# The hand-over from an RWKV scan to the FFN behind it: last output products from SBUF in eight PSUM banks, early tiles for the next stage, and a token norm in a written order

## The chip, the cores and the metric

The kernel runs on one core of a Trainium2 chip. Its time is the device time of one execution in microseconds (us), taken as the median of several runs. One further execution was taken with the hardware profiler; the traces below are of that one.

Engines: PE is TensorE (matrix products; PEld its weight loads), DVE is VectorE, ACT is ScalarE, POOL is GpSimd, SP is the engine whose queue issues all DMAs of this kernel. PSUM has eight banks of 128 x 512 float32.

## The reference

A trunk of two layers on 512 tokens of 1024 channels. Each layer is FFN, mixer, FFN, with a layer norm behind each of the three. The mixer of layer 0 is neighbourhood attention, that of layer 1 a bidirectional RWKV-7 scan. The change lies between the mixer of layer 1 and the last FFN:

```python
def layer_norm(x, g, b):
    mu = mean(x, -1); var = mean(square(x - mu), -1)
    return (x - mu) * rsqrt(var + 1e-5) * g + b

def swiglu(x, w_in, w_out):
    gate, up = split(x @ w_in, 2)          # F = 2816
    return (silu(gate) * up) @ w_out

# end of rwkv7_bidir: y is the scan's output, 16 heads of 64 channels
y = groupnorm(y) * lnx_g + lnx_b           # over the 64 channels of each head
m = ((y + bonus) * g) @ w_out              # (512 x 1024) @ (1024 x 1024)

x = layer_norm(ALPHA * x + m, ln_g[1], ln_b[1])
x = layer_norm(ALPHA * x + 0.5 * swiglu(x, w_in, w_out), ln_g[2], ln_b[2])
```

All data are float32. Most large products are made of three float32r products (`mm3`: high x high, high x low, low x high) on operands that `split` has cut in two: an ACT copy makes the high part and a subtraction on DVE or POOL the low part.

## The kernel before

**The scan.** Class `Scan` goes through the eight head pairs in slots numbered -2 to 7. In slot n pair n runs its chain of eight steps over the time chunks, while pairs n+1 to n+3 are prepared. Each part of the work is a generator with a letter: `c` is the chain (four yields a step), `d` the outputs of a step, `x` (`finish`, pair n-1) the group norm of a finished pair, `e` (`gate`, pair n-1) its gating, `o` (`outs`) the early output products, `v` the value projection, `i`, `k`, `j` the inversion of the chunk matrices, whose long part is a series of small POOL operations. The strings in `SEQ` say in which order the generators advance in a slot. Under `manual_schedule(engines=MANUAL_SCAN)` PE, ACT and DVE execute exactly in that order; POOL and the DMA queue of SP are ordered by the scheduler, and each executes in its order.

A chain step is: PE `c` (L1204), ACT `wr` (L1205), PE `c` (L1216), ACT `vt` (L1217, L1218), PE `m` (L1222), DVE `vt` (L1224).

**The output product.** `gate` writes each pair's gated output to the DRAM tensor `d_o`. In slots 6 and 7 `outs` takes the pairs 0 to 4 (`EARLY = 5`): it loads them into `xv` (the former value input), loads the matching rows of w_out into tiles that the scan no longer needs (`ar`, `ar`, `bk`, `bk`, `wv`, in that order), multiplies (`wide`, L849: one product in two halves of 64 columns), adds ALPHA * x and stores the sums to `d_x`.

**The hand-over.** After slot 7 come `finish(7)` and `gate(7)`. Then the pools of the scan are closed and `rwkv_out` runs, ordered by the scheduler: it reloads the last three pairs from `d_o`, loads and splits the last three row blocks of w_out, reloads x from `d_x`, makes the remaining products with `mm3` (72 products, L239), and normalises the four token tiles (`residual_norm`). `to_channels` transposes each normed tile (L277) and splits it into `xT` (the "put"). In between `lead` loads and splits four units of the FFN's first weights and multiplies them with the first half of the tokens; `follow` does the second half at the head of `ffn`. The unit loads of the FFN go through two `raw` buffers, the splits' low parts are on POOL (L197), and `Winograd.sums` (L639 to L642) prepares its second weights on POOL.

Lines of the norm: L295 adds the products to x and sums the rows, L299 and L300 are the variance and its root on ACT, L303 and L306 apply mean, gain, scale and bias on DVE.

## Time and profile before

| | before |
|---|---|
| runs | 2314.69, 2315.7, 2319.5 us |
| median | 2315.7 us |
| profiled execution | 2311.64 us |
| its span, first to last instruction | 2309.9 us |
| PE busy in the span | 2169.5 us (94%) |
| POOL busy in the span | 1442.0 us (62%) |
| DVE, ACT busy | 1107.9 us (48%), 983.0 us (43%) |
| mean granted clock of TensorE | 0.973 |

How to read the rows. In the windows view each row is a stretch in us from the span's start, its length, the busy time of each engine with the number of its instructions, the granted clock of TensorE (1.00 is full speed), the share of time that the DMA engines were busy, and GB/s. In the timeline a row is start, duration, engine, line, operation, what it writes and reads, and in brackets how long the engine was idle before and what ended that. In the chain of waits a row is start, duration, and what the end of the program was waiting for just then. A group row gives minimum, median and maximum in ns. Matrix products are pipelined: the duration of one is longer than the distance between two.

### The profile page before, as it was taken

Reading aid. Unit: us, or ns where it says so; the run is one execution under the profiler, and the core shown is the slowest. Engines: PE = TensorE matmul, PEld = TensorE weight load, DVE = VectorE, ACT = ScalarE, POOL = GpSimd, SP = SyncE. Lnnn points to the kernel's source line nnn. Section 1 sums busy time; section 2 is a strip of 40 time slices with the busy share of each in tenths; the row PEclk is TensorE's granted clock in tenths of the full one; section 3 lists DMA queues with packets and bytes.
Section 4 is the critical chain, followed back from the end, with each engine's and each line's share of the span. In section 5 each row is a group of like instructions: output and inputs, shape, how many; then the busy total and the mean of one; then the engine's idle time right before and its main releaser. Section 6 shows DMA issues by size and latency. Waiting matters only on the chain. (4 is left out here: it accounts for less than half of the span.)

```text
span 2309.9 us, 35198 instructions
## 1 busy us (share of the span) xinstructions
PE 2169.5 (94%) x13808; PEld 1716.6 (74%) x13808; DVE 1107.9 (48%) x1552; ACT 983.0 (43%) x1712; POOL 1442.0 (62%) x1231
## 2 busy tenths in 40 slices
PE   8999999999999999999999878799999876999998
PEld 7888878887888887888888655445666545888886
DVE  2333357375523335723333695435887446233336
ACT  3333335376333333533333434336777423333334
POOL 6778745465568775777886532145877506578863
PEclk9999999999999999999999979799999987999999
DMA  6444453432434446344445416744545426244453
GB/s 202 138 150 146 140 197 124 126 92 79 140 114 137 141 138 226 113 134 146 143 140 191 127 56 204 255 142 121 146 126 145 132 94 211 82 147 142 141 173 119
DMA packets 351362, 330.40 MB, mean 143 GB/s; under 512 B 48554, under 2 KB 277546, under 8 KB 351196
## 3 DMA queue, kind: packets, MB, share of 16 engines
q1 hardware_dynamic: 351196, 328.15, 45.3%
q8 instruction: 108, 1.77, 0.3%
q14 instruction: 58, 0.48, 0.1%
HBM read 263.05 MB, written 48.53 MB: 135 GB/s over the span
## 5 line engine op out<-in xcount | busy, mean ns | idle before, releaser
L197 POOL TENSOR_TENSOR w<-raw,w 128x1024 fp32r<-128x1024 f32 (+2 forms) x203 | 503.7, 2482 | 311.7 <-ACT w L196 306.3
L201 PE MATMUL bank<-xT,w 128*128 128x512 f32 x1416 | 552.4, 390 | 0.0
L202 PE MATMUL bank<-xT,w 128*128 128x512 f32 x1416 | 551.6, 390 | 0.0
L203 PE MATMUL bank<-xT,w 128*128 128x512 f32 x1416 | 551.5, 389 | 0.0
L196 ACT ACTIVATE w<-raw 128x1024 fp32r<-128x1024 f32 (+1 forms) x207 | 218.7, 1057 | 337.5 <-POOL ts L639 142.2
L347 DVE SCALAR_TENSOR_TENSOR ar<-bank,tmp 128x512 f32<-128x512 f32 x88 | 60.9, 692 | 588.8 <-PE bank L203 579.4
L203 PEld LDWEIGHTS bank<-xT,w 128*128 128x128 f32 x1416 | 266.1, 188 | 55.6
L202 PEld LDWEIGHTS bank<-xT,w 128*128 128x128 f32 x1416 | 266.2, 188 | 54.0
L201 PEld LDWEIGHTS bank<-xT,w 128*128 128x128 f32 x1416 | 266.1, 188 | 54.2
L668 PE MATMUL bank<-w,ring 128*128 128x512 f32 x864 | 200.8, 390 | 9.1 <-DVE w L197 8.0
L668 PEld LDWEIGHTS bank<-w,ring 128*128 128x128 f32 x864 | 161.6, 188 | 45.8 <-DVE w L197 10.6
L668 PE MATMUL bank<-wx,an 128*128 128x512 f32 x792 | 187.3, 389 | 0.0
L1143 POOL TENSOR_TENSOR tm<-qs,zs 128x126 f32<-128x126 f32 (+22 forms) x248 | 106.9, 431 | 106.4 <-DVE qs L1136 61.3
L668 PEld LDWEIGHTS bank<-wx,an 128*128 128x128 f32 x792 | 148.7, 188 | 30.8
L197 POOL TENSOR_TENSOR wx<-ra,wx 128x512 fp32r<-128x512 f32 x132 | 168.5, 1307 | 0.0
L197 DVE TENSOR_TENSOR ring<-ar,ring 128x1024 fp32r<-128x1024 f32 x44 | 130.8, 2972 | 72.7 <-ACT ring L196 72.5
L345 ACT ACTIVATE tmp<-bank 128x512 f32<-128x512 f32 x88 | 52.6, 598 | 240.6 <-PE bank L203 240.6
L1145 POOL TENSOR_TENSOR zs<-zs,tm 128x126 f32<-128x126 f32 (+22 forms) x248 | 113.5, 458 | 19.4
L196 ACT ACTIVATE wx<-ra 128x512 fp32r<-128x512 f32 x132 | 83.1, 633 | 86.0 <-PE bank L668 68.0
L197 POOL TENSOR_TENSOR w<-late,w 128x1024 fp32r<-128x1024 f32 x28 | 70.6, 2520 | 76.2 <-ACT w L196 69.2
L201 PE MATMUL bank<-xT,ring 128*128 128x256 f32 (+1 forms) x352 | 103.3, 308 | 10.6 <-ACT xT L196 8.7
L639 POOL TENSOR_TENSOR ts<-ra 128x512 f32<-128x512 f32 x44 | 57.6, 1309 | 86.2 <-DMA ra<-in_ffn_w_out_dram 86.1
(277 smaller groups left out, 3797.1 us busy)
## 6 DMA issues: line engine op xcount, KB each, us to landing
raw<-in_ffn_w_in_dram SPq DMA_DIRECT2D x176, 512.0 KB, 3.7
ra<-in_ffn_w_out_dram SPq DMA_DIRECT2D x44, 1024.0 KB, 4.9
late<-d_late SPq DMA_DIRECT2D x30, 512.0 KB, 5.3
late<-in_ffn_w_out_dram SPq DMA_DIRECT2D x28, 512.0 KB, 4.5
raw<-in_w_qkv_dram SPq DMA_DIRECT2D x24, 512.0 KB, 3.7
d_late<-ts SPq DMA_DIRECT2D x44, 256.0 KB, 3.2
d_late<-ra SPq DMA_DIRECT2D x44, 256.0 KB, 2.0
xs<-ar SPq DMA_DIRECT2D x64, 128.0 KB, 2.3
```

The costliest lines, as they stand in the source:

```text
L196: self.nc.scalar.activation(h, raw, AF.Copy)
L197: (eng or self.nc.vector).tensor_tensor(l, raw, h.bitcast(F32), ALU.subtract)
L201: nc.tensor.matmul(out, wh, xh, start=start, stop=False)
L202: nc.tensor.matmul(out, wh, xl, start=False, stop=False)
L203: nc.tensor.matmul(out, wl, xh, start=False, stop=stop)
L345: nc.scalar.activation(s, pg, AF.Silu)
L347: nc.vector.scalar_tensor_tensor(raw[:, 3:7:3] if j else raw[:, 0:8:7], halves_of(pu), 0.5, halves_of(s), ALU.mult, ALU.mult)
L639: nc.gpsimd.tensor_tensor(t3, r[:, 1, 1], r[:, 0, 1], ALU.subtract)
L668: self.nc.tensor.matmul(acc, lhs, u[:, i], start=bool(first) and m == 0, stop=last and m == 2, skip_group_check=more)
L1143: nc.gpsimd.tensor_tensor(tv, qs[:, s, 0:s].rearrange("p (a o) -> p a o", o=1).broadcast_to([P, s, n]), zs[:, s : s + 1, c0:].broadcast_to ...
L1145: nc.gpsimd.tensor_tensor(zs[:, 0:s, c0:], zs[:, 0:s, c0:], tv, ALU.add)
```

## The change

- `outs` starts with the tile `wv`, then the two `ar` and two `bk`, and also loads the row blocks 5, 6 and 7 of w_out into three unit tiles of the scan. In `SEQ[6]` the first `o` stands behind one whole chain step and the start of the next.
- From pair 5 on `gate` leaves its result in `xv` in SBUF instead of `d_o`.
- `last` replaces the products of `rwkv_out`: the pairs 5, 6 and 7 are multiplied in plain float32 (24 products), each half of a token tile in a PSUM bank of its own, eight in all. The products of pairs 5 and 6 for the first two tiles stand ahead of the gating of pair 7.
- The tiles that the scan does not need in its last slot lie in a pool of their own (`rwe`, tags `EARLY_TAGS`) on the other side of SBUF. It is closed ahead of slot 7, and a pool `ex` is opened in its place, for x, the norm parameters, the two `raw` buffers and four weight units of the next stage. A generator `leads` (letter `w` in `SEQ[7]`) loads and splits the four leading FFN units there in slot 7; x is reloaded as soon as both halves of a tile are stored (`reload`).
- `rwkv_out` keeps only the norm, cut into four steps for each tile, in a written order for PE, ACT and DVE.
- A POOL copy that reads the last scaled tile is the `mark`: all POOL work of the FFN is ordered behind it (`issue_after`).

```diff
-    6: "c x n o o c c o o x c o c c x c d n c o c c d c x o c o c x c c x d o c o c c c d o c n o o o o o c c d k c "
+    6: "c x n c c x c c o c x c o d n o o o c o c c d c x o c o c x c c x d o c o c c c d o c n o o o o o c c d k c "
        "o o o o o c o c k c d c j c d o c c j c o o d e o",
-    7: "x c c c o x c o c c d c o c o c c c x d o c o c c d c o c o c c d c x o c o c c d x c o c o c c d x c o c e "
-       "d c c c o d",
+    7: "w x c c c o x c o c c d c o c o c c c x d o c o c w c d c o c o c c d c x w o c o c c d x c o c w o c c d x c o c e "
+       "w d c c c o d",
...
+EARLY_TAGS = ("k", "iv", "r", "lw", "kz", "a2r", "a2u", "v", "vr", "qc", "qd", "zs", "qs", "tm")
...
     def raw(self):
-        return self.sb_w.tile([P, 1024], F32, name="raw", tag="raw", bufs=self.nraw)
+        return self.home(self.sb_w).tile([P, 1024], F32, name="raw", tag="raw", bufs=self.nraw)
...
-    def rwkv_out(self, x, o, w_out, ln, lead):
-        oT = self.new_xT()
-        units = []
-        for c in range(EARLY, ND):
-            raw = self.tmp()
-            self.nc.sync.dma_start(raw, o[:, c, :])
-            self.split(*oT.get(c), halves_of(raw))
-            units.append(self.load_unit(w_out[c * P : (c + 1) * P, :], None, True, self.nc.vector))
-        self.load_x(x)
-        params = self.ln_params(ln)
...
+    def rwkv_out(self, acc, params, lead):
+        self.spare.append(self.ring())
         nxt = self.new_xT()
...
+        banks = [(self.bank(), self.bank()) for _ in range(NT)]
+        def norm(t):
+            y, yn = self.x[t], [self.tmp() for _ in range(2)]
+            s0, s1, mu, va, rs, self.mark = self.small("st", 6)
+            for h, sm in zip(range(2), (s0, s1)):                       # sum step
+                stt(y[:, hs[h]], y[:, hs[h]], 1.0, acc[t][h], ALU.mult, ALU.add, accum_out=sm)
+            nc.vector.tensor_scalar(mu, s0, s1, -1.0 / D, ALU.add, ALU.mult)
+            nc.scalar.activation(self.junk.bitcast(BF16), y, AF.Square, bias=mu, accum_out=va)
+            nc.scalar.activation(rs, va, AF.Sqrt, scale=1.0 / D, bias=self.eps)
+            yield
+            for h in range(2):                                          # mean step
+                stt(yn[h], y[:, hs[h]], mu, gbc[:, hs[h]], ALU.add, ALU.mult)
+            yield
+            nc.vector.reciprocal(rs, rs)                                # scale step
+            for h in range(2):
+                stt(y[:, hs[h]], yn[h], rs, bbc[:, hs[h]], ALU.mult, ALU.add)
+            yield
+            self.to_channels(t, y, nxt, banks[t])                       # transposes and put
+            yield
...
+        with self.tc.manual_schedule(engines=MANUAL_SCAN):
+            order(0, 0, 1, 0, 1, 0, 1)
+            order(2, 1, 2)
+            parts = self.lead(lead, nxt)
+            next(parts)
+            order(2, 3, 3, 2, 3)
+            self.mark = nc.gpsimd.tensor_copy(self.mark, self.x[3][:, 0:1])
+            next(parts)
+            order(3)
         return nxt
...
+                if n == HEADS // 2 - 1:
+                    self.early.tile([P, 56], F32, name="pad")
+                    self.opened.close()
+                    late.enter_context(self.k.early())
+                    self.lw = self.leads(lead, ln)
                 self.slot(n)
-            list(self.finish(HEADS // 2 - 1))
-            list(self.gate(HEADS // 2 - 1))
+            self.ending = self.finish(HEADS // 2 - 1)
+            next(self.ending)
+    def leads(self, lead, ln):
+        k, nc = self.k, self.nc
+        nc.sync.dma_start(self.w[ND - 1], self.w_out[(ND - 1) * P :, :])
+        k.x = [k.ex.tile([P, D], F32, name=f"x{t}", tag="x", bufs=NT) for t in range(NT)]
+        self.params = k.ln_params(ln)
...
+        load(0)
+        load(1)
+        self.reload()
+        yield
+        for i in range(LEAD):
+            u = k.ring().rearrange("p (i f) -> p i f", i=2)
+            k.split(u[:, 0, :], u[:, 1, :], raws[i], nc.gpsimd)
...
+            if i + 2 < LEAD:
+                load(i + 2)
+            yield
+    def reload(self):
+        while self.k.ex and self.stored >= 2:
+            t = NT - len(self.left)
+            self.nc.sync.dma_start(self.k.x[t], self.left.pop(0))
+            self.stored -= 2
+    def last(self):
...
+        def add(t, h, cs):
+            if cs[0] == EARLY:
+                acc[t, h] = self.k.bank()
+            for c in cs:
+                nc.tensor.matmul(acc[t, h], self.xv[:, c, t * P : (t + 1) * P], self.w[c][:, h * 512 : (h + 1) * 512],
+                                 start=c == EARLY, stop=c == hp)
+        with self.k.tc.manual_schedule(engines=MANUAL_SCAN):
+            list(self.ending)
+            for t, h in ((0, 0), (0, 1), (1, 0), (1, 1)):
+                add(t, h, (EARLY, EARLY + 1))
+            list(self.gate(hp, "bank"))
+            add(2, 0, (EARLY, EARLY + 1))
+            for t, h in ((0, 0), (0, 1), (1, 0), (1, 1), (2, 0)):
+                add(t, h, (hp,))
+            for t, h in ((2, 1), (3, 0), (3, 1)):
+                add(t, h, (EARLY, EARLY + 1, hp))
...
-        w = [self.tile(n, [P, NC, 2, CH], 2).rearrange("p a b c -> p (a b c)") for n in ("ar", "ar", "bk", "bk")]
-        w += [self.tile("wv", [P, ND, P]).rearrange("p a b -> p (a b)"),
-              self.units[self.taken[5, 1][0]][0].rearrange("p a b c d -> p (a b c d)")]
+        w = [self.tile("wv", [P, ND, P]).rearrange("p a b -> p (a b)")]
+        w += [self.tile(n, [P, NC, 2, CH], 2).rearrange("p a b c -> p (a b c)") for n in ("ar", "ar", "bk", "bk")]
+        w += [self.units[i][0].rearrange("p a b c d -> p (a b c d)") for i in (2, 4, 3)]
...
-        nc.vector.scalar_tensor_tensor(bon, bon, k.col(C_XB, hp), g, ALU.add, ALU.mult)
-        nc.sync.dma_start(self.dram["o"][:, hp, :], bon)
+        early = hp < EARLY
+        nc.vector.scalar_tensor_tensor(bon if early else self.xv[:, hp, :], bon, k.col(C_XB, hp), g, ALU.add, ALU.mult)
+        if early:
+            nc.sync.dma_start(self.dram["o"][:, hp, :], bon)
...
+            with tc.issue_after(k.mark.ins):
+                k.ffn(xT, ffn_w_in[1, 1], ffn_w_out[1, 1], 5, lambda: None)
```

More of the change, by code (lines that the diff above doesn't have):

```diff
@@ L100, in __init__ @@
         self.nc = tc.nc
+        self.ex, self.spare = None, []
         nc = self.nc
@@ L216, in lead @@
     def lead(self, cols, xT):
-        us = [self.load_cols(w, c0, True) for w, c0 in cols]
+        us = [u if isinstance(u, bass.AP) else self.load_cols(*u, True) for u in cols]
         self.led = us, [self.bank() for _ in us], xT
@@ L595, in rwkv_project, with order @@
                 store(dram["g"][:, c, :], pp)
[L597 to L620 removed]
+    def rwkv_out(self, acc, params, lead):
+        self.spare.append(self.ring())
+        nxt = self.new_xT()
+        nc = self.nc
+        gbc, bbc = params
+        hs = [slice(h * 512, (h + 1) * 512) for h in range(2)]
+        stt = nc.vector.scalar_tensor_tensor
+        banks = [(self.bank(), self.bank()) for _ in range(NT)]
[17 more added lines that the diff above has]
+            yield
+        def order(*ts):
+            for t in ts:
+                next(ns[t])
+        self.junk = self.tmp()
+        ns = [norm(t) for t in range(NT)]
+        with self.tc.manual_schedule(engines=MANUAL_SCAN):
[7 more added lines that the diff above has]
+            order(3)
@@ L925, in take, with run @@
         return self.units[i]
-    def run(self):
+    def run(self, late, lead, ln):
         with self.k.tc.manual_schedule(engines=MANUAL_SCAN):
@@ L1264, in outs @@
                     nc.sync.dma_start(w[i], rows(self.w_out, i))
+                    for c in range(EARLY, ND - 1):
+                        nc.sync.dma_start(w[c], rows(self.w_out, c))
                 self.wide(acc, self.xv[:, i, t * P : (t + 1) * P], w[i][:, hs], i == 0, i == EARLY - 1)
@@ L1293, in finish, with gate @@
         yield
-    def gate(self, hp):
+    def gate(self, hp, bank="p"):
         k, nc = self.k, self.nc
```

107 lines of the change are left out of this document (77 added, 30 removed), and 1 row of the table SEQ.

## The prediction

> **What bounds the kernel now.** I read the page first, then the windows view with one row per stretch, then the chain of waits through the slowest stretch, then the timeline of single engines there.
>
> ```profile
> span 2309.9 us, 35198 instructions
> ```
> ```profile
> core 0: us, PE busy (x) PEld busy (x) DVE busy (x) ACT busy (x) POOL busy (x), PEclk, DMA share, GB/s
> 1851.00:1887.40 36.40, 35.91 (x628) 23.03 (x625) 15.13 (x41) 12.15 (x39) 0.00 (x0) 1.00 0.18 61
> 1887.40:1951.00 63.60, 25.92 (x103) 20.52 (x103) 40.14 (x67) 22.33 (x35) 30.27 (x16) 0.71 0.59 201
> 1951.00:1954.60 3.60, 3.60 (x18) 3.60 (x18) 3.60 (x5) 2.04 (x3) 2.59 (x1) 0.50 0.77 249
> 1951.00:1976.60 25.60, 25.35 (x196) 25.02 (x196) 6.74 (x9) 6.05 (x8) 5.75 (x3) 0.93 0.33 97
> 1976.60:2309.90 333.30, 323.01 (x1427) 266.93 (x1426) 134.28 (x129) 118.47 (x146) 225.65 (x136) 0.99 0.43 139
> ```
>
> TensorE fills the end of the scan (35.91 of 36.40 us) and the last FFN (323.01 of 333.30). Between them, from the last scan product at 1887.4 to the first dense FFN products at 1951, lie 63.6 us in which it is busy 25.92 us at a mean clock of 0.71. The 192 products of the FFN's four leading units then last to 1976.6. The chain says what fills the gap:
>
> ```profile
> 1887.37 0.61 ACT yt L1276
> ...
> 1894.09 1.10 PE p L1304 x4
> ...
> 1896.00 0.76 DVE bon L1306
> ...
> 1898.60 6.10 DMA raw<-in_rw_out_dram
> 1904.77 10.81 DMA ra<-in_ffn_w_out_dram
> ...
> 1924.22 3.87 DMA raw<-in_ffn_w_in_dram
> ...
> 1934.59 4.48 DVE x L306 x4
> 1939.07 7.19 DVE tmp L303 x3
> ```
>
> First the last head pair is normalised and gated (9.4 us, 1887.37 to 1896.76). Then come transfers that could not start before: the pair's output passes through DRAM, w_out's last rows are loaded and split, FFN weights arrive, one landing taking 10.81 us. Last come token norms with VectorE steps stretched. GpSimd had been idle for 83 us, and then works exactly beside the norms:
>
> ```profile
> 1915.74 1.27 POOL L639 TENSOR_TENSOR ts<-ra 128x512 f32<-128x512 f32 x1 [83.12 <-DMA ra<-in_ffn_w_out_dram]
> L303 DVE SCALAR_TENSOR_TENSOR tmp<-x,st,gbc x48: 739/752/2883, 353.3 to 2303.6; 128x512 f32<-128x512 f32 x48
> L295 DVE SCALAR_TENSOR_TENSOR x<-x,bank x8: 675/684/689, 1920.7 to 1927.6; 128x512 f32<-128x512 f32 x8
> ```
>
> L303 (two SBUF inputs) takes 0.75 us, up to 2.88 beside GpSimd; L295, with one input from PSUM, never over 0.69. So the stretch is bound by latency: no engine is full, and a shorter chain moves the end one for one.
>
> **Slot 6: when w_out's rows land.** The second early output product waits for its rows:
>
> ```profile
> 1807.78 1.08 PE L849 MATMUL a<-xv,wv 128*64 128x512 f32 x4
> 1811.96 1.03 PE L849 MATMUL a<-ar,xv 128*64 128x512 f32 x4
> 1812.92 0.39 SPq L1264 DMA_DIRECT2D wv<-in_rw_out_dram  x1
> 1814.01 0.33 SPq L1255 DMA_DIRECT2D ar<-in_rw_out_dram  x1
> 1819.86 1.97 PE L849 MATMUL a<-ar,xv 128*64 128x512 f32 x4 [6.87 <-DMA ar<-in_rw_out_dram]
> 1832.40 0.22 POOL L1145 TENSOR_TENSOR zs<-zs,tm 128x16 f32<-128x16 f32 x1
> 1845.19 5.53 SPq L1160 DMA_DIRECT2D az<-qd  x8
> raw<-in_ffn_w_in_dram SPq DMA_DIRECT2D x176, 512.0 KB, 3.7
> ```
>
> Its rows are issued at 1814.01, into a tile that the scan reads to the end of slot 5, and as the last of four such loads. The change starts with the rows that go into `wv`, read last at 1808.9, and moves the first `o` behind one whole chain step. Gone are the idle 6.87 us and the slow clock behind it (1.97 against 1.03 us, 0.94). What may be left is an estimated 1.5 us: the `wv` load, issued now at 1812.92, would move up by one place to about 1812.4 and land after 3.7; the shifted product is due one chain step (3.4 us, below) behind the start of the slot, less what stood there, at about 1814.6. I take 6.87 + 0.94 - 1.5 = **6.3 us gained**. The bounds are 0 (the stall only moves) and 7.8. The inversion on GpSimd, which this slot needs too, ends at 1832.4; what is made from it goes out by DMA only from 1845.2, so 6.3 us are covered. The outputs of the last three pairs no longer pass through DRAM, and the two extra row loads are queued behind and wanted only after the scan; both cost nothing here.
>
> **Slot 7: the lead work moved under the scan.** Four FFN units are now loaded and split here, with x, the norm parameters and w_out's last rows, at a DMA share of 0.18 and an empty GpSimd. Each split is an activation of 1.06 us and a GpSimd op of 2.4:
>
> ```profile
> L196 ACT ACTIVATE ring<-raw x7: 1042/1057/1062, 1902.2 to 1937.2; 128x1024 fp32r<-128x1024 f32 x7
> L197 POOL TENSOR_TENSOR ring<-raw,ring x28: 2336/2405/2951, 15.9 to 1938.4; 128x1024 fp32r<-128x1024 f32 x28
> 1871.51 0.28 ACT L1205 ACTIVATE wr<-c 128x128 f32<-128x128 f32 x1 [2.11 <-PE c L1204]
> 1872.35 0.27 ACT L1217 ACTIVATE vt<-c 64x128 f32<-64x128 f32 x1 [0.57 <-PE c L1216]
> 1881.68 0.28 ACT L1205 ACTIVATE wr<-c 128x128 f32<-128x128 f32 x1 [1.85 <-PE c L1204]
> 1885.18 0.75 DVE L1306 SCALAR_TENSOR_TENSOR bon<-bon,cols,gate 128x512 f32<-128x512 f32 x1
> 1888.00 0.69 DVE L1283 TENSOR_REDUCE sm<-yt 128x8 f32<-128x512 f32 x1 [0.32 <-ACT yt L1276]
> ```
>
> The first `w` that splits stands between `wr` and `vt` of one step, where ScalarE is idle 0.57 us: 1.06 - 0.57 = 0.5 us on the chain. The other three stand behind `vt`, where 1.85 us are idle, and cost nothing if their rows have landed; the last has the least room, since its load waits for a buffer that the second split gives back. The last GpSimd part runs about 1885 to 1887.4 beside L1306 (both inputs in SBUF); that ends about 2.2 us late, at 1888.2, L1268 (of L295's kind, 0.69) follows, and L1283 starts 0.9 us late, on the path. Together **1.4 us lost**, bounds 0 and 9.6 (four splits of 2.4 us, each holding VectorE up in full, as L303 was held up for 2.1). New waits on SP are those of the x loads for the stores of x; behind them stand only lead loads and the gates' operands, with a landing of 3.7 us; a step of the chain takes 3.4 (1871.51 to 1881.68 is three).
>
> [...]
>
> **The tail, from the end of the scan (t = 0 at 1887.37).** The prices:
>
> ```profile
> L239 PE MATMUL bank<-ring,xT x72: 387/389/795, 1903.3 to 1923.3; 128*128 128x512 f32 x72
> 1413.55 1.89 PE L541 MATMUL bank<-tmp 128*16 128x512 f32 x4
> 1963.91 1.03 PE L277 MATMUL bank<-ident,x 128*128 128x128 f32 x8
> 1961.75 0.28 PE L201 MATMUL bank<-xT,ring 128*128 128x256 f32 x1
> ...
> 1963.79 0.28 PE L203 MATMUL bank<-xT,ring 128*128 128x256 f32 x1
> L197 DVE TENSOR_TENSOR xT<-bank,xT x40: 674/683/692, 8.3 to 1965.8; 128x512 fp32r<-128x512 f32 x40
> L639 POOL TENSOR_TENSOR ts<-ra x44: 1269/1291/1742, 20.8 to 2208.1; 128x512 f32<-128x512 f32 x44
> ```
>
> Removed: the DRAM trip, three row splits and 72 split products. Added: 24 plain float32 products. Four records of such products take 1.89 us, that is 0.43 each behind a start of 0.17; a product makes two, so 0.86 us and 24 x 0.86 = 20.6 us. That row has 16 weight columns. The other near row, L849, does the same 128x512 product in two halves of 64 in 1.03; the 14 products on the path would then add 2.4 us. I take 0.86, since the new products come in one piece.
>
> Eight products run while the last pair is normalised (t 0 to 6.9; its transposes are due at 6.7, and at full clock win the 0.2 back: four took 1.10, eight take 1.03 below), two more beside the gate. From 9.4, 14 remain: the first token tile's sums are complete by 11.1, all by 9.4 + 14 x 0.86 = **21.4**. The first two tiles' sums and mean steps on VectorE hide in this.
>
> Then TensorE and VectorE alternate. Prices: 8 transposes 1.03; put, two subtractions of 0.68 behind an activation of 0.6 (that of L1276); sum step two of L295, 1.35; mean step two of L303, 1.5; scale step the same and a reciprocal, an estimated 0.15, 1.65.
> - Transposes of tile 0 to 22.5, its put to 24.1 on VectorE; scale of tile 1 to 25.8; sum of tile 2 to 27.1; put of tile 1 to 28.8.
> - Part 1 starts at 28.8. The two matmul rows are the first and the last of 18, so 0.12 us apart: 48 x 0.12 = 5.8, and 1.8 for the clock: to 36.4.
> - VectorE meanwhile: mean of 2, scale of 2, sum and mean of 3, to 34.8. Transposes of tile 2 to 37.4, put to 39.0, scale of 3 to 40.7; the held GpSimd is released near 40.
> - Part 2, 37.4 to 43.2; transposes of tile 3 to 44.2; first half of its put at 45.0; follow, 96 x 0.12 = 11.5, to **56.5**.
>
> Before, this point was 1976.6 - 1887.4 = 89.2. **Gain 32.7 us.** Of the uncertain terms, the clock costs 0 to 3.6, float32 0 to 2.4, GpSimd's release 0 to 9 (below), unseen hand-over latency 0 to 5.
>
> The clock: in the row 1951.00:1954.60 it is 0.50 after a gap. Here 7.4 us lie between the last product (21.4) and part 1 (28.8), with one burst of transposes between. I charge half of 3.6 us. [...]
>
> GpSimd after its release at 40 has seven ops of 1.29 us for the first pair of the FFN (9.0) and the first further unit (2.4), ready at 51.5; TensorE wants that at 56.5. With VectorE in the way (1.74 each) it is 54.6. Later in the FFN it is busy 225.65 of 333.30 us and catches up, so I cost the hold at nothing.
>
> The scan's start, where tiles now lie elsewhere and may become free earlier or later, is taken as 0, bounds -3 and +3: nothing of it shows in the trace before.
>
> **Sum**: -6.3 + 1.4 - 32.7 = -37.6 us. The profiled execution took 2311.64 us (span 2309.9); the runs shown were 2314.69, 2315.7 and 2319.5. Applied to their median: 2315.7 - 37.6 = **2278 us**. This kernel's measurement can tell about 0.2% (4.6 us) from no change.
>
> **Rivals.**
> - *The slot 6 stall only moves*, so the change does not do that part: the rows still wait for tiles of the last pair and crowd each other. For it: four loads of 512 KB meet there either way. Against: `wv` is free before the last pair's tiles. Time 2278 + 6.3 = 2284. Chance 0.10.
> - *VectorE is blocked in slot 7* by all four splits as L303 is now: 9.6 instead of 0.9 us, 2287. Against: of the VectorE work there, the chain's own step and the sums read PSUM, as L295 does. Chance 0.10.
> - *GpSimd becomes the bound* after its hold, if the second pair's sums are queued ahead of the next unit: 51.5 + 9.0 + 2.4 = 62.9 against 56.5, and a second such wait of the same size: 2278 + 13 = 2291. For it: the hold starts all its FFN work at 40. Against: its load of two thirds. Chance 0.08.
> - *Slower*: ScalarE's order is fixed, so a lead split whose rows have not landed stops the scan's chain. If SP is held at the x loads or by tiles not yet free, four loads of L us, each with 1.06 and 2.4 for its split, and both gates' operands behind them, run one after another: 6 L + 13.8, less the 15.9 us from that first `w` (1871.5) to the end of the scan. At the 10.81 us seen in a crowd that is 62.8 us lost, in place of the 1.4: 2278 + 61.4 = 2339. It eats the whole gain from about L = 6.9 us on. Against: DMA share 0.18 there, two buffers, 3.7 us for such a load. Chance 0.07.
>
> **How the numbers follow.** The forecast has 0.62 (2268 to 2289 with its bounds), mixed cases up to 2302 have 0.03. The range 2268 to 2302 leaves out the slow case and the ends. Faster by over 0.2% is the forecast, three rivals and most of the mixed cases: 0.91; within 0.2%: 0.02; slower: 0.07.
>
> **What would show it.** Right: no wait of 6.87 us on w_out rows in slot 6; GpSimd with four lead splits before the scan's end; 24 products with two records each in place of L239's 72; about 57 us from the last pair's L1276 to the end of the 192 lead products; L303 and L306 near 0.75 us in this tail. Wrong: ScalarE waiting in slot 7 for `raw`; TensorE waiting for a GpSimd split behind the follow products; a longer gap at the start of the scan.

## The result, and the profile after

The changed kernel takes 2283.28 us (median of 4 runs, 2278.77 to 2286.32), the kernel before 2317.09 us (4 runs, 2314.69 to 2319.5): a ratio of 0.9852, 95% interval 0.9831 to 0.9874. It is 33.8 us faster; 37.6 were forecast. The profiled execution took 2285.11 us.

The windows view of after, cut at the same events as before: the last 36.4 us of the scan, then up to the first lead products, through these, and the rest.

```profile
span 2283.0 us, 35114 instructions
```
```profile
core 0: us, PE busy (x) PEld busy (x) DVE busy (x) ACT busy (x) POOL busy (x), PEclk, DMA share, GB/s
1857.50:1893.90 36.40, 34.20 (x511) 20.59 (x508) 17.44 (x38) 14.16 (x38) 9.43 (x4) 0.95 0.52 171
1893.90:1922.70 28.80, 23.65 (x68) 10.96 (x68) 18.42 (x47) 11.07 (x19) 0.00 (x0) 0.95 0.26 91
1922.70:1951.00 28.30, 27.86 (x213) 27.15 (x214) 11.96 (x23) 8.66 (x14) 15.63 (x11) 0.93 0.32 102
1951.00:2283.00 332.00, 321.81 (x1419) 265.82 (x1417) 132.40 (x129) 118.46 (x146) 233.77 (x142) 0.99 0.44 145
```

The 63.6 us in which TensorE was busy 25.92 have become 28.8 us with 23.65. The four GpSimd splits (9.43 us) now lie under the scan. The row that holds them shows something new: before, TensorE was busy 35.91 of the last 36.40 us of the scan at clock 1.00, now 34.20 at 0.95. The chain of waits of after shows both places:

```profile
1818.42 4.29 DMA wv<-in_rw_out_dram
1822.76 1.98 PE a L889 x4
...
1859.35 0.31 PE c L1340 x5
1859.66 1.79 issue
1861.45 0.41 PE c L1340 x3
1861.86 3.43 PE a L889 x8
...
1893.82 7.06 PE bank L1054 x16
1900.88 0.44 PE bank L1433 x4
1901.32 13.92 PE bank L1054 x32
1915.23 0.45 PE bank L298 x4
```

In the tail no transfer is left: TensorE's products, one after the other, then transposes. But in slot 6 TensorE stops for 1.79 us after five of eight products of one line, with nothing that the profile could name as releaser ("issue"). In the timeline of after, at the end of slot 6:

```profile
1854.11 0.44 SPq L284 DMA_DIRECT2D gbc<-in_ln_g_dram  x1
1854.59 0.46 SPq L284 DMA_DIRECT2D bbc<-in_ln_b_dram  x1
1858.10 0.28 ACT L1329 ACTIVATE wr<-c 128x128 f32<-128x128 f32 x1 [0.88 <-PE c L1328]
1859.28 0.38 PE L1340 MATMUL c<-wr,az 64*64 64x64 f32 x5
1861.45 0.41 PE L1340 MATMUL c<-wr,az 64*64 64x64 f32 x3 [1.79 <-issue]
1861.79 3.50 PE L889 MATMUL a<-bk,xv 128*64 128x512 f32 x8
1867.61 0.28 ACT L1329 ACTIVATE wr<-c 128x128 f32<-128x128 f32 x1 [0.72 <-PE c L1328]
```

Eight output products that take 1.89 to 1.94 us elsewhere in this slot take 3.50 behind the stop (the clock there is 0.50), and from the last wr copy of slot 6 to the first of slot 7 it is 9.51 us; before, 5.86.

By stretches, from the profiled execution of each kernel (us). "2 steps" is from the first to the third wr copy (line 1329; before, 1205) of slot 6, "end" from its eighth to the first of slot 7, "slot 6" the whole, "slot 7" from there to the last pair's yt copy (L1405; before, L1276), "tail" from that to the first product of the FFN's second matmul (L708; before, L668), which lies 10.5 us behind the end of the 192 lead products in after, 10.4 in before. The medians come from several chips; the ratios in the text are always to the kernel before on the same chip.

| kernel | median | 2 steps | end | slot 6 | slot 7 | tail |
|---|---|---|---|---|---|---|
| before | 2317.09 | 18.23 | 5.86 | 49.02 | 26.11 | 100.34 |
| after | 2283.28 | 14.90 | 9.51 | 49.34 | 26.25 | 67.05 |
| after again | 2283.57 | 14.63 | 8.53 | 48.08 | 26.26 | 67.13 |
| no hold | 2290.35 | 15.88 | 9.96 | 50.76 | 26.26 | 73.98 |
| leads in the tail | 2295.63 | 15.03 | 11.35 | 51.31 | 26.12 | 75.34 |
| rows in the old tiles | 2285.70 | 19.21 | 7.64 | 51.78 | 26.25 | 67.22 |
| products after the gate | 2294.27 | 16.35 | 10.31 | 51.59 | 26.27 | 76.80 |
| loads late | 2279.85 | 12.85 | 5.86 | 43.65 | 27.34 | 67.47 |
| gbc, bbc late | 2279.34 | 15.29 | 5.86 | 46.07 | 26.27 | 67.27 |
| loads in turn | 2282.10 | 16.49 | 5.86 | 47.28 | 26.91 | 67.19 |
| norm order | 2274.44 | 15.64 | 9.67 | 50.24 | 26.26 | 60.59 |
| in turn, norm order, leads split up | 2273.97 | 14.78 | 5.85 | 45.56 | 27.25 | 60.07 |
| the same, row first | 2271.68 | 11.97 | 5.86 | 42.75 | 27.72 | 60.07 |
| combined | 2269.03 | 13.23 | 5.85 | 44.00 | 26.26 | 60.07 |

So from before to after slot 6 gives +0.3, slot 7 +0.1, the tail -33.3: together -32.8, against -33.8 between the medians. The profiled pair differs by less, 26.5 us, because after was 6.0 us late already at the start of slot 6 (1818.27 against 1812.24 us). That need not be an effect of the change: the thirteen profiles that share after's order up to slot 6 have the first wr copy of the scan anywhere from 1578.6 to 1588.6 us. Before has it at 1579.6, but its profiled execution is 5.5 us below its median, and it was profiled only once, so a few us at the scan's start, either way, are not excluded.

### The profile page after: what moved, and what is told of

It reads as the page before. It is cut to its first block, busy times and chain, and to the rows that moved or that the text cites. A ratio compares the mean times of both kernels' runs of the same rounds, so it can differ in the third digit from the quotient of the medians.

```text
span 2283.0 us, 35114 instructions
## 1 busy us (share of the span) xinstructions
PE 2179.1 (95%) x13784; PEld 1715.7 (75%) x13784; DVE 1099.8 (48%) x1546; ACT 978.0 (43%) x1706; POOL 1434.4 (63%) x1232
## 3 DMA queue, kind: packets, MB, share of 16 engines
q8 instruction: 108, 1.77, 0.3%
## 5 line engine op out<-in xcount | busy, mean ns | idle before, releaser
L708 PE MATMUL bank<-w,ring 128*128 128x512 f32 x864 | 201.2, 390 | 10.8 <-DVE w L217 10.2
L708 PEld LDWEIGHTS bank<-w,ring 128*128 128x128 f32 x864 | 161.5, 188 | 47.9 <-DVE w L217 13.2
L708 PE MATMUL bank<-wx,an 128*128 128x512 f32 x792 | 187.3, 389 | 0.0
L708 PEld LDWEIGHTS bank<-wx,an 128*128 128x128 f32 x792 | 148.7, 188 | 30.8
L217 POOL TENSOR_TENSOR ring<-raw,ring 128x1024 fp32r<-128x1024 f32 x28 | 70.2, 2516 | 96.3 <-ACT ring L216 96.0
```

Of the source, the lines that this page charges most:

```text
L217: (eng or self.nc.vector).tensor_tensor(l, raw, h.bitcast(F32), ALU.subtract)
L708: self.nc.tensor.matmul(acc, lhs, u[:, i], start=bool(first) and m == 0, stop=last and m == 2, skip_group_check=more)
```

## The experiments

**What the tail's parts are worth.** Three kernels each take one part out.

```diff
-            with tc.issue_after(k.mark.ins):
+            if True:
...
-            self.mark = nc.gpsimd.tensor_copy(self.mark, self.x[3][:, 0:1])
```


> The changed kernel with the hold and its marker copy taken out, so that GpSimd may start the last FFN's subtractions as soon as their data land. Theory (what the hold is for in the trace of after): the two-input VectorE steps of the norm (lines 637 and 641, 0.75 us each now) meet a 2.35 us GpSimd subtraction and take up to 2.4 us, as lines 1421 and 1436 did in slot 7 (2.38 and 2.26 us). With two to four such meetings, 1.6 us each, the stretch from the last yt copy (line 1405) to the last lead product grows from 56.6 us to 60-63 us, and the kernel by 0 to +6 us, less what the FFN gains by having its first weights split early. Rival: the meetings fall beside steps with a PSUM operand or into VectorE's waits, the stretch stays at 56.6 us within 1 us and the hold is worth nothing; the FFN may then even end 1-3 us earlier.

2290.35 us (2289.21 to 2296.23), ratio 0.9888 (0.9863 to 0.9912). The tail is 73.98 us, 6.9 longer than in after, and the rest of the FFN is hardly shorter (321.7 us behind L708's first product; after 322.1). VectorE and GpSimd of this kernel, start, duration, engine and line:

```profile
1898.68 2.37 POOL L217 TENSOR_TENSOR w<-raw,w 128x1024 fp32r<-128x1024 f32 x1 [0.26 <-ACT w L216]
1898.88 2.19 DVE L201 SCALAR_TENSOR_TENSOR sm<-sm 128x8 f32<-128x8 f32 x1
...
1915.22 4.51 DVE L637 SCALAR_TENSOR_TENSOR tmp<-x,st,gbc 128x512 f32<-128x512 f32 x2
1916.38 2.79 POOL L217 TENSOR_TENSOR w<-raw,w 128x1024 fp32r<-128x1024 f32 x1
```

In these rows a VectorE step with two SBUF inputs that meets a GpSimd subtraction ends only behind it: the pair of L637 takes 4.51 us instead of 1.42, and even a step on 8 columns, 0.17 us alone, takes 2.19. The hold is worth 6.9 us, just above the upper end of the theory. Not all of it need be these meetings: TensorE also spends 3.41 us more of this tail at half clock than in after.

```diff
-        load(0)
-        load(1)
         self.reload()
         yield
-        for i in range(LEAD):
-            ...
+        self.led = list(lead)
```


> The changed kernel with the four lead units neither loaded nor split in slot 7, but loaded and split by the norm stage as before the change; everything else (products from SBUF in eight banks, tile-by-tile norm, hold) stays. Theory of my sum: the four units cost slot 7 almost nothing (26.25 us with them, 26.1 without) and their absence is felt in the tail: four loads of 512 KB that start when raw buffers are free and four splits (ACT about 1.1 us and a subtraction of 1-2.4 us each) stand ahead of the lead products and among the norm's ACT and VectorE steps; the stretch from the last yt copy to the last lead product grows from 56.6 us to 63-72 us. Rival: raws are loaded early all the same, the splits find room before the first lead products are possible (about 29 us after the yt copy), and the stretch stays within 2 us of 56.6; the early units are then worth nothing, and slot 7 shows 26.1 us.

2295.63 us (2293.02 to 2300.88), ratio 0.9906 (0.9876 to 0.9937). Slot 7 is 0.13 us shorter without the splits, the tail 8.3 us longer, as the theory had it. In this kernel's timeline TensorE waits for the splits and ScalarE for the rows:

```profile
1928.88 0.58 PE L221 MATMUL bank<-xT,ring 128*128 128x256 f32 x1 [4.33 <-ACT ring L216]
1931.63 0.58 PE L223 MATMUL bank<-xT,ring 128*128 128x256 f32 x1 [1.96 <-POOL ring L217]
1936.40 1.06 ACT L216 ACTIVATE ring<-raw 128x1024 fp32r<-128x1024 f32 x1 [6.64 <-DMA raw<-in_ffn_w_in_dram]
```

```diff
-            for t, h in ((0, 0), (0, 1), (1, 0), (1, 1)):
-                add(t, h, (EARLY, EARLY + 1))
             list(self.gate(hp, "bank"))
-            ...
+            for t, h in ((t, h) for t in range(NT) for h in range(2)):
                 add(t, h, (EARLY, EARLY + 1, hp))
```


> The changed kernel with all 48 records of last-row products behind the transposes of the last gate, instead of 16 of them ahead of it (7.13 us beside the last normalisation of VectorE). Theory of my sum, in which TensorE's 21 us of products stand on the path up to the first transposes of tile 0: these come 7.1 us later and with them the first lead product (36 us after the last yt copy, not 28.9) and the end of the lead products, kernel +7 us. Rival: the put waits for VectorE as much as for TensorE (it idles 4.5 us there, but tile 0's own products are ready only 1.7 us later), so only 2 to 4 us are lost. Nothing else changes.

2294.27 us (2290.41 to 2299.06), ratio 0.9903 (0.9887 to 0.9919). The first transposes of tile 0 come 30.45 us behind the yt copy, not 21.2, and the tail is 9.7 us longer: the 7.1 us of the theory and 2 to 3 more. These fit the clock: beside the normalisation TensorE is busy 0.36 of 7.00 us at a mean clock of 0.64, and the first products run at 0.50:

```profile
1898.00:1905.00 7.00, 0.36 (x2) 0.36 (x3) 5.39 (x18) 3.23 (x4) 0.00 (x0) 0.64 0.53 161
1905.00:1909.00 4.00, 4.00 (x9) 1.93 (x8) 1.50 (x2) 0.00 (x0) 0.00 (x0) 0.50 0.94 374
```

So the early products save time twice.

**Where slot 6's gain went.** First, the rows' places of before in the changed kernel. The expectation speaks of the old order of slot 6 as well, but the kernel that ran keeps after's `SEQ[6]`; only the rows' tiles are those of before:

```diff
-        w = [self.tile("wv", ...)]
-        w += [self.tile(n, ...) for n in ("ar", "ar", "bk", "bk")]
+        w = [self.tile(n, ...) for n in ("ar", "ar", "bk", "bk")]
+        w += [self.tile("wv", ...)]
```


> The changed kernel with slot 6 in the order of before and the five w_out rows in the old places (ar, ar, bk, bk, wv). Theory: the first three steps of slot 6 (from the first wr copy, line 1329, to the third) go back from 14.9 us to 18.2 us, since the products of the last rows wait for their load again, and the rest of the slot, including the gap before slot 7 (9.5 us from the last wr copy of slot 6 to the first of slot 7, against 5.9 us before), stays as it is, so slot 6 takes 52.6 us and the kernel is 3.3 us slower than after. Rival: the 3.6 us at the end of slot 6 are the same delay moved (the products that were taken out of the start are done at the end); then the last gap goes back to 5.9 us and slot 6 takes 49 us, no change.

2285.70 us (2283.85 to 2286.94), ratio 0.9862 (0.984 to 0.9884). The wait is back and two steps take 19.21 us, so moving the first `o` does not remove the wait by itself; it takes the start with `wv` as well:

```profile
1827.33 1.97 PE L889 MATMUL a<-ar,xv 128*64 128x512 f32 x4 [4.80 <-DMA ar<-in_rw_out_dram]
```

The end stays long, with the same stop inside L1340 (1.56 us), although the start is slow again. Since the order of the products was not put back, this run does not test the rival that products moved out of the start lengthen the end; the runs below do, with the same order and no stop. In time this kernel and after cannot be told apart, 1 to 3 us being within their spread.

Then the loads with which slot 7 begins, all held behind the store of slot 6's end (`self.put` is the last store of `outs`):

```diff
-        nc.sync.dma_start(self.w[ND - 1], self.w_out[(ND - 1) * P :, :])
...
-        self.params = k.ln_params(ln)
-        raws = {}
+        with k.tc.issue_after(self.put):
+            nc.sync.dma_start(self.w[ND - 1], self.w_out[(ND - 1) * P :, :])
+            self.params, raws = k.ln_params(ln), {}
...
-        load(0)
-        load(1)
-        self.reload()
+        with k.tc.issue_after(self.put):
+            load(0), load(1)
+            self.reload()
...
-            nc.sync.dma_start(rows(self.dram["x"], t)[:, hs], x)
+            self.put = nc.sync.dma_start(rows(self.dram["x"], t)[:, hs], x).ins
```


> The changed kernel with the loads that slot 7 begins with (the last w_out row, gbc and bbc, two raws, the first x tiles, 3.5 MB in all) held on the load queue behind the store of line 1396 that in after went out at 1866.06 us, so that they run during the first steps of slot 7 and not during the last steps of slot 6. Theory: TensorE's 1.79 us gap in the middle of line 1340 and the half clock after it come from those loads (its instructions arrive late beside them); from the last wr copy of slot 6 to the first of slot 7 falls from 9.5 us to 5.9-7 us, and a gap of the same kind may show in slot 7 instead (26.25 us now), or none; kernel -3.6 us to 0. Rival: the gap belongs to this place in TensorE's program, whatever the loads do; it stays at 1.5-2 us and 9.5 us, and slot 7 does not change. If the raws land too late for the first split, slot 7's first ACT split waits and slot 7 grows.

2279.85 us (2274.05 to 2282.43), ratio 0.9834 (0.9807 to 0.986). The stop is gone, the end is 5.86 us as before, and slot 6 takes 43.65 us. Slot 7 is 1.1 us longer: its third split waits 1.77 us for a late raw. The loads now run beside slot 7, denser than ahead of the stop, and no such stop appears there. A window of after, ahead of the stop, and one of this kernel:

```profile
1856.00:1858.00 2.00, 2.00 (x36) 1.29 (x36) 0.58 (x2) 1.18 (x2) 0.00 (x0) 1.00 0.81 221
1862.00:1864.00 2.00, 2.00 (x42) 1.50 (x40) 1.68 (x5) 0.82 (x3) 0.00 (x0) 1.00 1.18 362
```

So it is not the crowd as such. Two queues of the DMA view are listed as "instruction": q8 with 108 packets and 1.77 MB in after, that is blocks of 16 KB, and q14 with 57 and 0.47 MB. In this kernel a block of q8 lands at about 1863.8, in the middle of the loads, and TensorE does not stop. The half microsecond in which the block in question moves, first in after (1859.0 to 1859.5), then in before (1853.0 to 1853.5):

```profile
q1 hardware_dynamic: 21, 0.06, 30.5%
q8 instruction: 1, 0.02, 11.0%
```
```profile
q8 instruction: 1, 0.02, 11.7%
```

Against the last wr copy of slot 6 the block lands about 1 us behind in after (its packet starts at 1859.06 and takes 0.88 us, the copy starts at 1858.10) and 2 us ahead in before (1853.33 and 0.93; 1855.40); the start of the packet is what is compared. In all seven profiles with gbc and bbc in front of it (after twice, and the experiments that leave these loads) it lands 0.4 to 2.0 us behind the copy, and TensorE stops inside L1340, behind the fifth of its eight products, for 1.56 to 2.55 us. In the seven others, before among them, it lands some 2 us ahead and there is no stop. To narrow it down, gbc and bbc alone were held:

```diff
-        self.params = k.ln_params(ln)
+        with k.tc.issue_after(self.put): self.params = k.ln_params(ln)
```


> The changed kernel with gbc and bbc alone (1 MB, issued at 1854.1 and 1854.6 us in after) held behind the store that ends slot 6; the raws, the last w_out row and x stay where they are. Theory: the instruction block that TensorE misses is due about 2.4 us ahead of the last wr copy of slot 6, when of all loads just these two are in flight; without them it lands in time, the stop inside line 1340 (1.56 to 2.55 us in six profiles) is gone, 5.9 us from that copy to slot 7, and the kernel is 3.6 us below after. Rival: any 3 MB there do it (raws and x too, which are issued from 1859.4 us on); then the stop stays, perhaps shorter, and the gap is 8-9.5 us.

2279.34 us (2278.17 to 2283.33), ratio 0.9838 (0.9824 to 0.9852): no stop, 5.86 us from the last wr copy to slot 7, and slot 7 as in after:

```profile
1857.35 0.45 PE L1340 MATMUL c<-wr,az 64*64 64x64 f32 x8
1862.02 0.28 ACT L1329 ACTIVATE wr<-c 128x128 f32<-128x128 f32 x1 [0.72 <-PE c L1328]
```

This is the theory: 1 MB of loads is enough. The order of the products is that of after, so it is not the moved start either. Beside it on the same chip after itself:

> The changed kernel itself once more, beside the last version on the same chip, to see how far its stretches repeat. Theory: the stop inside line 1340 is there again (1.5-2.6 us, 9.5-11.4 us from the last wr copy of slot 6 to slot 7), the half clock at the start of slot 6 nearly always (14.8-16.5 us for two steps), so slot 6 takes 49-52 us, as in before or up to 3 us more, and the tail repeats within 0.3 us (67 us to the first FFN result). Rival: the stop is a matter of one run's chance; then it is absent here and slot 6 takes 45-46 us.

2283.57 us (2280.82 to 2287.09), ratio 0.9858 (0.9842 to 0.9873): the stop is there (2.45 us) and the tail repeats within 0.1 us. The end is 8.53 us, below the 9.5 expected, because here the clock stays at 1.00 behind the stop. The kernel with gbc and bbc late is 4.2 us below it, though the runs of the two overlap.

**Versions.** Raws and the last w_out row behind the store, the rest behind later stores:

```diff
-        self.params = k.ln_params(ln)
...
-        load(0)
-        load(1)
-        self.reload()
+        with k.tc.issue_after(self.put):
+            load(0), load(1), nc.sync.dma_start(self.w[ND - 1], self.w_out[(ND - 1) * P :, :])
         yield
         for i in range(LEAD):
+            with k.tc.issue_after(self.put):
+                for t, g in zip(self.params, (k.ln_g, k.ln_b)) if i == 0 else ():
+                    nc.sync.dma_start(t, ...)
...
-            self.reload()
+            with self.k.tc.issue_after(self.put): self.reload()
```

> The changed kernel with the loads of slot 7's start taken apart: the first two raws and the last w_out row behind the store that ended slot 6 (line 1396), x, gbc and bbc behind the next stores. Theory (shown so far by one run with all of them behind that store: TensorE's gap gone, slot 6 43.7 us, slot 7 27.3 us): TensorE's instruction block lands some 2.4 us ahead of the last wr copy of slot 6 and not 0.4-1.6 us behind it, no gap, 5.9 us from that copy to slot 7; slot 6 43.5-46 us; and with the raws first the first ACT split waits less, slot 7 26.2-26.8 us. Kernel 5 to 6 us below after, about 2278 us. Rival: the short start of slot 6 in that run (12.85 us for two steps, full clock) was chance, as the order there is the same; then it is 14.9-15.9 us again, slot 6 takes 46 us, and the kernel is about 3.5 us below after.

2282.10 us (2276.9 to 2286.09), ratio 0.9848 (0.9831 to 0.9865). The stop is gone, but two steps take 16.49 us, so the short start with all loads late was chance, as the rival had it, and slot 7 is 0.7 us longer than in after. In time it cannot be told from after.

```diff
-            order(0, 0, 1, 0, 1, 0, 1)
-            order(2, 1, 2)
+            order(0, 0, 0, 1, 1, 0, 1, 1)
+            order(2, 0, 1, 2, 2)
...
-            order(2, 3, 3, 2, 3)
+            order(2, 3, 3, 3, 2, 3)
```
(The sums and the activations of a token tile are two steps here.)

> The changed kernel with VectorE's order in the norm alone altered: the last step of tile 1 and the sums of tile 2 stand ahead of the first put, where VectorE idles 4.52 us in the profile of after (from 1911.8 to 1916.3, until TensorE has ended its 32 products and transposed tile 0). Theory: from there VectorE's chain of steps sets the time (put of tile 1, lead products, last put, follow), so 3.2 us of its work moved into the idle time bring the first lead product from 28.9 to 25.5 us after the last yt copy and the end of the lead products 3 us forward; kernel -3 us. Rival: TensorE sets the time behind the first lead product (it has 24 us of lead products to do and the transposes between them); then the first lead product comes 3.4 us earlier, but the end moves by 0 to 2 us only. Slot 6 and slot 7 are as in after (49-51 and 26.2 us).

2274.44 us (2273.72 to 2277.17), ratio 0.9818 (0.9805 to 0.9832). The tail falls by 6.5 us, twice what the theory had. The first lead product comes 23.47 us behind the yt copy, 5.4 earlier (3.4 expected): with tile 1 scaled in VectorE's idle time both tiles' 16 transposes run as one block, and with them their copies and puts:

```profile
1913.94 1.91 PE L298 MATMUL bank<-ident,x 128*128 128x128 f32 x16
1914.58 2.07 ACT L216 ACTIVATE xT<-bank 128x512 fp32r<-128x512 f32 x4 [4.87 <-PE bank L298]
1915.21 2.49 DVE L217 TENSOR_TENSOR xT<-bank,xT 128x512 fp32r<-128x512 f32 x4 [1.53 <-ACT xT L216]
```

My own sum had followed the order of the diff, and left this wait in. The other 1.1 us fit the clock, which no longer falls there. The same stretch of the tail in after and in this kernel:

```profile
1919.00:1927.00 8.00, 5.09 (x25) 4.24 (x24) 5.81 (x14) 2.51 (x5) 0.00 (x0) 0.57 0.01 2
1913.00:1921.00 8.00, 7.09 (x52) 6.04 (x51) 6.40 (x13) 3.49 (x7) 0.00 (x0) 1.00 0.01 2
```

All nine profiles of the changed kernel with the old order of the norm have 6.83 us or more at half clock in the tail; the four with the new order have none.

Both together, with the last put ahead of the fourth lead unit:

```diff
-            next(parts)
...
             order(3)
+            self.proj(lead[3], self.led[1][3], nxt, 0)
```

> The kernel with the loads in turn, the altered order of the norm, and the last put ahead of the fourth lead unit instead of behind all four, so that its copies run beside TensorE's products. Theory: slot 6 and slot 7 as with the loads in turn (43.5-46 and 26.2-26.8 us); from the last yt copy to the first result of the FFN (67 us in after) 3 us less by VectorE's order and 1-2 us less as the second halves of the lead products no longer wait for the last put: 62-63 us. Kernel 9 to 11 us below after, about 2273 us. Rival: TensorE's clock or its own work sets the end, 65-67 us as before, and the kernel equals the one with the loads in turn.

2273.97 us (2266.3 to 2279.77), ratio 0.9811 (0.979 to 0.9832). The splitting of the leads gave 0.5 us, not 1 to 2, and slot 7 took 27.25 us, not 26.2 to 26.8.

Then the row that slot 6's first output product needs is loaded ahead of the others (gbc and bbc move to `i == 2`):

```diff
-            nc.sync.dma_start(w[i], rows(self.w_out, i))
+            with self.k.tc.issue_after(ins[0]) if i == EARLY - 2 else nullcontext(): ins += [...]
...
+                with self.k.tc.issue_after(self.put) if (n, i) == (1, 0) else nullcontext():
+                    [nc.sync.dma_start(w[c], rows(self.w_out, c)) for c in range(EARLY, ND - 1) ...]
```


> The kernel with the loads in turn, the altered norm order and the lead units split up, and besides the w_out row that the first output product of slot 6 waits for (into wv) issued ahead of the two rows into bk and of the two into the free units, which now wait for the first store of the slot; gbc and bbc go behind the third raw. Theory: TensorE's half clock at the start of slot 6 (0.50 for 4 to 6 us in eight of nine profiles with this order, 1.00 only where the slot took 12.85 us for two steps) comes from its idle wait for that row, which lands 4.3-4.8 us after its issue; issued alone it lands in 3-3.7 us, the wait of 0.3-1.7 us is gone, the clock stays, and the first two steps take 12.2-13.5 us and not 14.8-16.5. Slot 6 43-44 us, slot 7 26.3-26.7 us, first FFN result 60 us after the yt copy; kernel 2-4 us below the one without, about 2271 us. Rival: the clock falls from the thin work of those steps, whatever the row does; then two steps take 14.5-15.5 us and the kernel stays at 2274 us.

2271.68 us (2267.27 to 2276.61), ratio 0.9801 (0.9786 to 0.9816). No wait for the row, clock 1.00 throughout, two steps in 11.97 us. Slot 7 loses 1.5 us: its last split waits 2.45 us for a late raw.

> What the runs point to, together: the w_out row into wv first, the rows into the free units behind the slot's first store, gbc and bbc behind the store that ends slot 6, the raws and x where the change had them, the altered norm order and the lead units split up. Theory: the stretches add up without touching each other: slot 6 42.7-43.0 us (first two steps 12.0 us at full clock, 5.9 us from its last wr copy to slot 7, no stop inside line 1340), slot 7 26.3 us (the row-first version had 27.7, its last raw being late), first FFN result 60.1 us after the yt copy; against after that is -5 to -6.5 us in slot 6 and -7 us in the tail, so 2270 to 2272 us, 1 to 2 us below the row-first version. Rival: with the other loads of slot 6 pushed back, the raws and x now meet the instruction block; then the stop is back (1.5-2.5 us, 9 us to slot 7) and the time is 2274 us.

2269.03 us (2267.71 to 2271.13), ratio 0.9806 (0.978 to 0.9831): with the one before, the fastest; the two are not told apart. There is no stop. But the clock fell at the start of slot 6 although no product waited for a row (two steps in 13.23 us, not 12.0), so there the rival of the row-first run holds in part:

```profile
1816.50:1817.00 0.50, 0.48 (x7) 0.38 (x8) 0.50 (x1) 0.26 (x1) 0.50 (x1) 1.00 1.02 418
1817.00:1817.50 0.50, 0.26 (x6) 0.12 (x4) 0.25 (x2) 0.42 (x1) 0.42 (x2) 0.70 1.00 410
1817.50:1818.00 0.50, 0.37 (x4) 0.33 (x4) 0.44 (x3) 0.20 (x1) 0.42 (x2) 0.50 1.06 426
```

## Why the prediction was right, and which step was not

The sign, the place and roughly the size of the total are right, because the tail carries it and the tail's mechanism held. The term for slot 6 failed by 6.6 us; slot 7 cost 1.3 us less than charged and the tail gave 0.6 more, which by luck brings the total closer. By stretches that is -32.8 us, and the medians, which scatter by some us, say -33.8.

*Tail, -32.7.* Measured from the yt copy to the end of the lead products: 56.6 us, forecast 56.5. (The same point of before was taken at 1976.6 us; its last lead product only starts at 1977.14, so the gain is 33.3.) The terms inside held too: products complete at 21.3 us (forecast 21.4), the first lead product at 28.9 (28.8). The prices:

```profile
L1054 PE MATMUL bank<-xs,xv x48: 592/592/697, 1893.7 to 1914.6; 128*128 128x512 f32 x48
L637 DVE SCALAR_TENSOR_TENSOR tmp<-x,st,gbc x8: 742/746/752, 1906.0 to 1929.0; 128x512 f32<-128x512 f32 x8
L641 DVE SCALAR_TENSOR_TENSOR x<-tmp,st,bbc x8: 747/750/755, 1909.1 to 1933.8; 128x512 f32<-128x512 f32 x8
```

Each of the 48 product records lasts 0.592 us, but they overlap: 32 of them span 14.08 us, 0.44 each, where 0.43 was taken, and the alternative with 2.4 us more fell away. For the clock 1.8 us were charged, by an estimate of mine that half of the 3.6 us seen at 0.50 in before would be lost; no run shows that share by itself. In after the half clock reaches 3.7 us into the lead products, so about 1.9 us are lost there (28.3 us at 0.93 in the windows view). The hold was costed at nothing: from L708's first product to the end it is 322.1 us, before 322.2. GpSimd did not become the bound.

*Slot 7, +1.4.* Measured +0.14. The 0.5 us for the split between wr and vt was 0.15: one step takes 3.42 us instead of 3.27. The 0.9 us for VectorE did not reach the path:

```profile
1891.02 2.36 POOL L217 TENSOR_TENSOR ring<-raw,ring 128x1024 fp32r<-128x1024 f32 x1 [1.18 <-ACT ring L216]
1891.67 2.26 DVE L1436 SCALAR_TENSOR_TENSOR xv<-bon,cols,gate 128x512 f32<-128x512 f32 x1
1893.85 0.67 DVE L1395 SCALAR_TENSOR_TENSOR e<-e,g 128x512 f32<-128x512 f32 x1
1894.49 0.69 DVE L1412 TENSOR_REDUCE sm<-yt 128x8 f32<-128x512 f32 x1
```

L1436 takes 2.26 us beside GpSimd's 2.36 (before, L1306 took 0.75) and ends behind it, as forecast, but that is at 1893.9, and L1412 follows the yt copy (1893.86, 0.60 us) at once. The rivals of slot 7 did not come: ScalarE waited for a raw once, 0.3 us.

*Slot 6, -6.3.* This step failed; measured +0.3. The wait of 6.87 us is gone, as said. But two sizes inside were wrong and one cost was missing. First, the products' row takes 4.29 us to land, where 3.7 was taken, and the slow clock, which was to go with the wait, stayed. It was priced at 0.94 us by one row, but in before it is 0.50 for 6.83 us; in the twelve profiles with the new order and the new tiles it is 0.50 for 6.83 us in seven, for 3.41 in three, and never in two. So in after two steps became 3.3 us shorter, not 6.3. In the two where the clock stayed at 1.00 they took 11.97 and 12.85 us, and 18.23 - 11.97 = 6.3: the total fits a start at full clock, though its parts were not measured singly. Second, the loads of slot 7 were costed by ScalarE, GpSimd and SP's queue only. With gbc and bbc among them TensorE also stops, and the end of slot 6 is 3.65 us longer (9.51 against 5.86), in none of my bounds. The rival that the stall only moves gives the same number, 2284 us, but is not what happened: the row's wait is gone, and the long end goes away when one pair of loads is moved, with the order of the products unchanged.

That this instruction block is TensorE's is inferred from the place and time of the stop; the trace does not name the owner of the queue. The counts fit it: q8 carries 108 blocks in both kernels, and TensorE executes 27616 products and weight loads in before and 27568 in after, some 255 for each block, while the other engines together have under 4500 instructions on the profile's page. Whether the first raws or x would do the same in that place was not tried; gbc and bbc are special in that each spreads one row over all partitions.

In seven profiles TensorE did not stop there; in the seven others the stop was 1.56 to 2.55 us, and in five of these the clock fell behind it.

*Scan start, 0.* No effect stands out from a scatter of 10 us, with one profile of before to compare with.

## What to carry to other kernels

When loads are moved under a stretch that a busy engine bounds, look in the trace for where instruction blocks arrive and keep bulk loads (here a pair that spreads rows over all partitions) off the microseconds ahead of them: here that took away a stop of 1.56 to 2.55 us. An "issue" gap in the middle of a run of equal instructions was the sign. Of the 6.3 us forecast for the removed wait, 3.3 came in after, with the clock at 0.50 for 6.83 us, and 5.4 and 6.3 in the two profiles where it stayed at 1.00, so put the gain at half clock into the sum too. When a tail has become a chain, look for the engine that idles in it and move a later tile's steps there: 6.5 us for a few lines of order.

## What the hardware showed that was not expected

- TensorE stopped in the middle of eight equal products, at the same one in seven profiles, when 1 MB of loads was issued 1 to 2 us ahead of the time at which an instruction block lands otherwise (block 0.4 to 2.0 us behind the last wr copy instead of some 2 us ahead, stop 1.56 to 2.55 us). Beside denser loads in slot 7 (362 GB/s against 221) it did not stop.
- The granted clock fell to 0.50 with no idle gap of TensorE over 0.92 us in the 3 us before it (the combined kernel), and with the same instructions and no wait it stayed at 1.00 in another (the row-first kernel); the runs do not show why. In windows of 0.2 us every whole stretch at half clock from 1800 to 1990 us, in all fourteen profiles, lasts 3.41 us or a multiple of it, up to 17.07: in before 6.83, 17.07, 13.65 and 10.24 us, in after 6.83, 3.41 and 6.83. The start of slot 6 in the combined kernel and in after, with full clock at both ends of each row:

```profile
1816.50:1821.00 4.50, 4.11 (x40) 2.79 (x40) 2.86 (x9) 1.17 (x3) 3.87 (x9) 0.62 1.01 377
1820.00:1828.00 8.00, 7.24 (x53) 3.65 (x53) 3.37 (x10) 1.99 (x6) 6.82 (x16) 0.57 0.95 357
```

Here 4.50 x (1 - 0.62) x 2 is 3.4 us at half clock, and 8.00 x (1 - 0.57) x 2 is 6.9.
- A VectorE step of 0.17 us on 8 columns took 2.19 us beside a GpSimd subtraction of 2.37 in the kernel without the hold, and ended with it (1901.07 against 1901.05 us).
